# A gating layer whose three products are made of half products, with its gate mixed in place

## The chip, the cores and the metric

The kernel runs on one core of one Trainium2 chip. The metric is the device time in microseconds of one execution. Before the change the median of three runs was 1120.9 us (1119.94 to 1122.56).

## The reference

Two layers with a residual stream x of 512 tokens by 1024 features, all in float32. Layer 0 is latent attention, layer 1 a gating layer; behind each stands an MLP with a squared ReLU. The gating layer and the MLP, cut to what matters:

```python
def chunked_sgu_mixer(h, w_in, ln_g, ln_b, w_spatial, b_spatial, w_out):
    z = gelu(h @ w_in)                  # 512x1024 @ 1024x4096
    u, v = split(z, 2, axis=-1)         # 512x2048 each
    v = layer_norm(v, ln_g, ln_b)
    # per 128-token chunk and group of 256 features: lower-triangular 128x128
    mixed = einsum('gts,bcsgd->bctgd', tril(w_spatial), v in chunks) + b_spatial
    return (u * mixed) @ w_out          # 512x2048 @ 2048x1024

x = x + chunked_sgu_mixer(rms_norm(x, norm_mix[1]), ...)
x = x + square(relu(rms_norm(x, norm_ffn[i]) @ w_up)) @ w_down
```

## The kernel before

Every float32 operand of a large product is split into a high part, rounded to the matmul's float32r format, and a low part, the rest. `split` (L124) does it: the high part is a cast on ScalarE (L125), the low part a subtraction on VectorE (`low`, L122). `mm3` (L106, the matmul is L110) makes a product from three matmuls: high by high, high by low, low by high. `wtiles` hands out the tiles for the split weights, three pairs in turn (`wh`, `wl`), `raw_tile` the shared buffers in which weights land (`wr`, two of 1 MB).

**The MLPs** (`ffn`) multiply by the Winograd form of Strassen's method: a product of two matrices cut into four quarters each is made of seven half-size products instead of eight, from sums of quarters. On the left these sums are made by VectorE (`Quarters.first` and `.rest`, L313 on: turn by transposes on TensorE, L296, copies on ScalarE and VectorE, L323 and L324, sums, splits). Sums of weights are made by DMA: a block is loaded by SP's queue (`load`, L1017) and another is added into the same buffer by a DMA on POOL's queue (`add`, L1020), or by VectorE where both lie in memory (L1049, L1264). `ffn` has six weight buffers: the two `wr` and four of its own (`wb`). The up product and the down product of 1024 hidden columns are seven items each; an item is a pair `prepare` (weights and splits) and `go` (24 products of 512 columns, or 48 of 256, then what takes the banks away). The list `work` deals the items of an up product and of the down product before it alternately; the last seven down items of the first MLP stand alone. `prepare` of an item is called two items ahead of its `go`. Sums that run on in a bank (X) are added to x, or to the hidden values, while the next item already writes the other bank of the pair. During an MLP's first item the other half of its input is turned, by way of two spare banks.

**The gating layer** does not do so. For v it goes over four blocks of 512 columns (L1381 on, four banks, two weight units of 512x512 each), takes Gelu on ScalarE (L1407) and statistics on VectorE (L1408). For u there are 16 tiles of 128 features (`u_tile`), made transposed: the product, a multiplication by the norm spread over a row (`rb`, L1424), Gelu. `mixed_tile` (L1428) mixes v along the positions by four short matmuls (L1431), scales and shifts (L1436), multiplies with u and splits the result into `hid`. `gate_pieces` multiplies two such tiles with 256 rows of `w_out` in eight pieces and adds them to x (L1457). `Features` turns and splits the layer's input in two halves (`gx1`), the first at the end of the first MLP. The weights of the position mixing come by four DMAs on POOL's queue behind the norm's root (`mix_load`).

The order of instructions on each engine is made by the framework from the program's order and its dependences; an engine then takes them strictly in that order. The tile pools of the layer and of the MLPs lie in the same memory one after the other.

Of the kernel before, what the change touches and what calls it, by code (L numbers as in the profile page):

```python
# [57 lines left out]
def trunk(ctx: ExitStack, tc: tile.TileContext, a):  # L58
# [240 lines left out]
    class Features:  # L299


        def __init__(self, key, base, halves=(0, 1)):
            self.g = [gcol(key, base + k) for k in range(KD)]
            self.t = [None] * KD
            self.halves = halves
            self.left = list(halves)

        def half(self):
            h = self.left.pop(0)
            for k in range(h * 4, h * 4 + 4):  # L310
                self.t[k] = split_scaled(gpair(), turned(k), self.g[k])

    class Quarters:  # L313
# [3 lines left out]
        def __init__(self, key, base):  # L317
            self.g = [gcol(key, base + k) for k in range(KD)]

        def turn(self, e, lo, hi):  # L320
            for k in range(4):
                ps, g = turned(e * 4 + k), self.g[e * 4 + k]
# [669 lines left out]
    def ffn(layer, xq, norm, pool, after=None, last=None):  # L992
# [21 lines left out]
        spare += banks[6:8]  # L1014

        def load(t, src):
            nc.sync.dma_start(t, src)  # L1017

        def add(t, src):
            nc.gpsimd.dma_start(t, src, accum_op=ALU.add)  # L1020
# [143 lines left out]
        def down(c, sq):  # L1164
# [59 lines left out]
            def item(left, weights, sums, first, then, free=False, free_left=False, late=None):  # L1224
# [19 lines left out]
                def go():  # L1244
                    l, r = w
                    for b in range(2):
                        bs = slice(b * P, (b + 1) * P)
                        for k in range(4):
# [4 lines left out]
                            )  # L1253
                    it, u, r, done = then
# [8 lines left out]
            def t2():  # L1263
# [9 lines left out]
                item(lambda: "a22", p4, "X", False, (1, 0, r2, True), True, True),  # L1273
# [14 lines left out]
        for j, (_, go) in enumerate(work):  # L1288
            if j == 7:
# [24 lines left out]

    def after_mlp0(i, u):
        norm1.add(i, u)
        if (i, u) == (3, 0):
            gx1.half()
# [8 lines left out]
    gx = gx1.t  # L1327
    norm2 = Norm(1)
    gx2 = Quarters("norm_ffn", KD)
    with stage(7), tc.tile_pool(name="sgu", bufs=1) as sg:  # L1330
# [5 lines left out]
        v = sg.tile([P, NT, SGW], F32, name="v")  # L1336
# [3 lines left out]

        def staged(i):
            return v[:, 2 * i : 2 * i + 2, SGW - 512 :].rearrange("p a (b t) -> p a b t", t=P)
# [3 lines left out]
        bs_src = a["sgu_b_spatial"].rearrange("l g t -> (l g t)")  # L1348
        def mix_load():
            for gg in range(2):  # L1350
                nc.gpsimd.dma_start(wsp[:, gg], ws_src[:, gg * 4 : gg * 4 + 4, :])
                nc.gpsimd.dma_start(
                    v[:, 2 + gg, SGW - 512 :], bs_src[gg * 512 : (gg + 1) * 512].partition_broadcast(P)
# [27 lines left out]
        for c in range(4):  # L1381
            acc = [psum() for _ in range(NT)]
            for at, kk in enumerate(gx1.halves):
                wh, wl = unit(wview(w_in, kk * 512, 512, SGW + c * 512, 512), 4, 512)
                for i in range(NT):
                    isl = slice(i * P, (i + 1) * P)
                    for k4 in range(4):
                        k = kk * 4 + k4
                        mm3(
                            acc[i], (gx[k][0][:, isl], gx[k][1][:, isl]),  # L1390
                            (wh[:, k4, :], wl[:, k4, :]), at + k4 == 0, at * 4 + k4 == KD - 1,
                        )
                if at == 0 and c == 0:
                    gx1.half()
# [218 lines left out]
```

## Time and profile before

| | |
|---|---|
| median of 3 runs | 1120.9 us |
| profiled execution | 1121.37 us, span 1119.6 us |
| TensorE busy | 1086.3 us, 97% of the span |
| VectorE busy | 815.5 us, 73% |
| ScalarE busy | 565.9 us, 51% |
| POOL busy | 103.5 us, 9% |
| granted clock of TensorE, mean | 0.992 of 2.4 GHz |

How to read it: a matmul's listed time (390 ns for 512 columns) overlaps with the next; what one costs is the distance from start to start. The span is the first to the last instruction of the profiled execution, and its time is that span and what lies around it. The first MLP runs from about 171 to 500 us, the gating layer to about 786 us, the second MLP to the end.

### The profile page before, as it was taken

Reading aid. Unit: us, or ns where it says so; the run is one execution under the profiler, and the core shown is the slowest. Engines: PE = TensorE matmul, PEld = TensorE weight load, DVE = VectorE, ACT = ScalarE, POOL = GpSimd, SP = SyncE. Lnnn points to the kernel's source line nnn. Section 1 sums busy time; section 2 is a strip of 40 time slices with the busy share of each in tenths; the row PEclk is TensorE's granted clock in tenths of the full one; section 3 lists DMA queues with packets and bytes.
Section 4 is the critical chain, followed back from the end, with each engine's and each line's share of the span. In section 5 each row is a group of like instructions: output and inputs, shape, how many; then the busy total and the mean of one; then the engine's idle time right before and its main releaser. Section 6 shows DMA issues by size and latency. Waiting matters only on the chain.

```text
span 1119.6 us, 15248 instructions
## 1 busy us (share of the span) xinstructions
PE 1086.3 (97%) x6348; PEld 958.6 (86%) x6348; DVE 815.5 (73%) x949; ACT 565.9 (51%) x668; POOL 103.5 (9%) x137
## 2 busy tenths in 40 slices
PE   8799998999999999989999999999899999999997
PEld 6688888999999999877888888888799999998986
DVE  6988757897887888964347566568788788788753
ACT  4577636665655655554223222223675555555641
POOL 5510000001010010001000000000000001001000
PEclk9999999999999999999999999999999999999999
DMA  6121147768758768253323133223966976866431
GB/s 199 40 75 38 39 113 238 176 150 195 180 137 210 199 124 220 68 136 113 107 82 112 43 109 113 76 76 76 263 161 144 223 187 122 218 150 113 114 113 57
DMA packets 80739, 148.63 MB, mean 133 GB/s; under 512 B 4694, under 2 KB 18589, under 8 KB 80541
## 3 DMA queue, kind: packets, MB, share of 16 engines
q1 hardware_dynamic: 56588, 99.41, 26.3%
q0 software_dynamic: 24080, 48.24, 24.7%
q8 instruction: 50, 0.82, 0.3%
q14 instruction: 21, 0.16, 0.0%
HBM read 145.54 MB, written 2.10 MB: 132 GB/s over the span
## 4 chain that ended last, share of the span: by engine, by line
PE 81%; DVE 5%; DMA 5%; issue 4%; ACT 3%; POOL 0%; SPq 0%; POOLq 0%; ACTq 0%; DVEq 0%
PE ps L110 76%; DVE wl L122 2%; ACT wh L125 2%; DMA wb<-in_ffn_w_down 2%; DMA wr<-in_ffn_w_up 2%; DMA wb<-in_ffn_w_up 2%; PE ps L1431 1%; PE ps L863 1%; DVE sq L492 1%; ACT p L843 0%; PE ps L296 0%; PE ps L830 0%; PE ps L831 0%; PE ps L834 0%; PE ps L832 0%
## 5 line engine op out<-in xcount | busy, mean ns | idle before, releaser
L110 PE MATMUL ps<-g,wh 128*128 128x256 f32 (+1 forms) x2112 | 420.9, 299 | 4.4 <-DVE g L122 2.7
L110 PEld LDWEIGHTS ps<-g,wh 128*128 128x128 f32 x2112 | 339.3, 190 | 22.1 <-DVE g L122 3.6
L110 PE MATMUL ps<-g,wl 128*128 128x256 f32 (+1 forms) x1056 | 314.0, 298 | 0.6 <-DVE wl L122 0.6
L110 PE MATMUL ps<-wh,q 128*128 128x512 f32 (+1 forms) x840 | 266.2, 389 | 2.5 <-DVE x L1160 2.5
L122 DVE TENSOR_TENSOR wl<-wr,wh 128x2048 fp32r<-128x2048 f32 (+1 forms) x74 | 165.0, 2232 | 57.8 <-ACT wh L125 57.7
L110 PEld LDWEIGHTS ps<-g,wl 128*128 128x128 f32 x1056 | 199.3, 189 | 7.2 <-DVE wl L122 0.9
L122 DVE TENSOR_TENSOR wl<-wb,wh 128x2048 fp32r<-128x2048 f32 x64 | 146.6, 2290 | 65.3 <-ACT wh L125 65.2
L110 PEld LDWEIGHTS ps<-wh,q 128*128 128x128 f32 x840 | 158.0, 189 | 34.6 <-issue 2.8
L125 ACT CAST wh<-wr 128x2048 fp32r<-128x2048 f32 (+1 forms) x74 | 137.4, 1860 | 98.4 <-PE ps L110 90.2
L125 ACT CAST wh<-wb 128x2048 fp32r<-128x2048 f32 x64 | 122.0, 1906 | 102.1 <-PE ps L110 85.7
L110 PE MATMUL ps<-wl,q 128*128 128x512 f32 (+1 forms) x420 | 163.6, 390 | 0.0
L125 ACT CAST q<-sq 128x1024 fp32r<-128x1024 f32 x51 | 53.6, 1052 | 90.1 <-PE ps L110 87.5
L110 PE MATMUL ps<-wh,g 128*128 128x512 f32 x304 | 96.0, 393 | 2.0 <-ACT g L134 1.7
L110 PEld LDWEIGHTS ps<-wl,q 128*128 128x128 f32 x420 | 79.5, 189 | 14.6
L1160 DVE SCALAR_TENSOR_TENSOR x<-ps,s,x 128x512 f32<-128x512 f32 x98 | 72.6, 747 | 21.8 <-PE ps L110 21.8
L110 PE MATMUL ps<-wh,h 128*128 128x512 f32 (+1 forms) x216 | 84.7, 392 | 0.0
L110 PE MATMUL ps<-wl,h 128*128 128x512 f32 (+1 forms) x216 | 82.5, 382 | 0.0
L110 PE MATMUL ps<-wh,l 128*128 128x512 f32 (+1 forms) x216 | 82.5, 382 | 0.0
L110 PEld LDWEIGHTS ps<-wh,g 128*128 128x128 f32 x304 | 56.9, 188 | 14.9 <-ACT g L134 2.2
L122 DVE TENSOR_TENSOR q<-sq,q 128x1024 fp32r<-128x1024 f32 x51 | 62.4, 1223 | 4.9 <-ACT q L125 1.8
L110 PE MATMUL ps<-wl,g 128*128 128x512 f32 x152 | 59.2, 389 | 0.0
L1020 POOL DMA_DIRECT2D wr<-in_ffn_w_up x16 | 20.9, 1309 | 408.8 <-DVE x L1457 183.2
(229 smaller groups left out, 1229.3 us busy)
## 6 DMA issues: line engine op xcount, KB each, us to landing
wb<-in_ffn_w_up SPq DMA_DIRECT2D x18, 1024.0 KB, 6.4
wb<-in_ffn_w_down SPq DMA_DIRECT2D x17, 1024.0 KB, 5.2
wb<-in_ffn_w_down POOLq DMA_DIRECT2D x17, 1024.0 KB, 9.4
wr<-in_ffn_w_up POOLq DMA_DIRECT2D x16, 1024.0 KB, 8.4
wr<-in_sgu_w_in SPq DMA_DIRECT2D x16, 1024.0 KB, 5.6
wr<-in_ffn_w_up SPq DMA_DIRECT2D x14, 1024.0 KB, 5.5
wr<-in_ffn_w_down SPq DMA_DIRECT2D x9, 1024.0 KB, 5.1
wb<-in_ffn_w_up POOLq DMA_DIRECT2D x8, 1024.0 KB, 8.4
```

The source lines that it names most:

```text
L110: nc.tensor.matmul(out, lhsT=lhsT, rhs=rhs, start=start and t == 0, stop=stop and t == 2, **kw)
L122: return eng.tensor_sub(l, src, h.bitcast(F32))
L125: nc.scalar.copy(hl[0], src)
L492: nc.vector.tensor_tensor_reduce(out=junk, in0=x[:, i, cuts[c] * P : cuts[c + 1] * P], in1=x[:, i, cuts[c] * P : cuts[c + 1] * P], scale=1 ...
L863: nc.tensor.transpose(ps[b][:, c : c + P], pr[h, i][:, j * P : (j + 1) * P], ident)
L1020: nc.gpsimd.dma_start(t, src, accum_op=ALU.add)
L1160: nc.vector.scalar_tensor_tensor(out=xs, in0=ps, scalar=r[:, i : i + 1], in1=xs, op0=ALU.mult, op1=ALU.add)
L1431: nc.tensor.matmul(ps[:, i * P : (i + 1) * P], lhsT=v[:, i, j * P : (j + 1) * P], rhs=wt[:, j // 2, :], start=True, stop=True,)
```

## The change

All three products of the gating layer are made of seven half-size products, as in the MLPs. `Quarters` takes which half of the features comes first and gives the layer's input too (`Features` goes); its first half is turned in the middle of the first MLP's last item (`mid`). `gate(c)` makes 1024 columns of v, `other(c)` 1024 features of u, `outer` the product with `w_out`, whose seven products have two items each, one for each half of the inner dimension. That is 42 items, one list, with `prepare` two ahead, seven items of one product behind one another. The layer has three weight buffers: the two `wr` and one `wb`; two more come from v for the output. v is normalised on ScalarE (scale and bias), mixed in place, and u is multiplied by it in place (`gated`). At an MLP's beginning four banks are spare for the transposes, from its second item on two.

```diff
+        def __init__(self, key, base, first=0):
+            self.halves = (first, 1 - first)
...
-        spare += banks[6:8]
+        spare += banks[4:8]
...
-                return wview(w_up, k * 512, 512, c * 1024 + i * 512, 512)
+                return wview(w_up, xq.row(k), 512, c * 1024 + i * 512, 512)
...
+                        if b == 0 and mid is not None:
+                            mid()
...
+            if j == 1:
+                spare[:] = banks[6:8]
...
-    gx1 = Features("norm_mix", KD, (1, 0))
+    gx1 = Quarters("norm_mix", KD, 1)
...
-        ffn(0, gx0, norm, fp, after_mlp0)
+        ffn(0, gx0, norm, fp, norm1.add, None, gx1.first)
...
+        raws = Slots(
+            [raw_tile((P, 4, 512)) for _ in range(2)] + [sg.tile([P, 4, 512], F32, name=nm("wb"))]
+        )
+        banks = [psum() for _ in range(8)]
+        B, A, C, E = (banks[2 * n : 2 * n + 2] for n in range(4))
...
+        def weights(w, name, make, free, shift=0):
+
+            make()
+            w.extend(split(wtiles(4, 512, shift), s[name]))
+            if free:
+                raws.put(s.pop(name))
...
+            def p1():
+                if c:
+                    get("a", w(0, 0))
+                add(s["a"], w(0, 1))
+
+            def p2():
+                nc.vector.tensor_add(s["a"], s["a"], s["b"])
...
+            return [
+                item(X, True, "A11", "d" if c else "a",
+                     lambda: get("d" if c else "a", w(0, 0)), bool(c), end1),
+                item(Z, True, "A12", "c", lambda: get("c", w(1, 0)), True, end2),
+                item(Y, True, "N1", "a", p1, False, end5),
+                item(Y, False, "S4", "b", lambda: get("b", w(1, 1)), False, end3, p2),
+                item(X, False, "S2", "a", lambda: None, False, end6),
+                item(X, False, "S3", "b", lambda: add(s["b"], w(0, 1)), True, end7),
+                item(X, False, "A22", "a", lambda: add(s["a"], w(1, 0)), True, end4),
+            ]
...
+            def p1():
+                get("a", w(1, 0))
+                add(s["a"], w(1, 1))
...
+            return [
+                cols_item(X, True, "A11", "b", lambda: get("b", w(0, 0)), False, end1),
+                cols_item(Y, True, "S3", "a", p1, False, end5),
+                cols_item(Z, True, "A12", "c", lambda: get("c", w(0, 1)), True, end2),
+                cols_item(X, False, "S2", "a", p2, False, end6),
+                cols_item(X, False, "N1", "b", lambda: add(s["b"], w(1, 0)), True, end7),
+                cols_item(Y, False, "A22", "a", lambda: add(s["a"], w(0, 1)), True, end3),
+                cols_item(X, False, "S4", "c", lambda: get("c", w(1, 1)), True, end4),
+            ]
...
+        def gated(c, name):
+            t, m = int(name[1]) - 1, int(name[2]) - 1
+            u = uq[c][name].rearrange("p j (i t) -> p j i t", i=2)
+            nc.vector.tensor_mul(
+                u, u,
+                v[c][:, 2 * t : 2 * t + 2, m * 512 : (m + 1) * 512].rearrange(
+                    "p i (j t) -> p j i t", j=4
+                ),
+            )
...
+            product(X, True, "a11", "a", put("a", 0, 0), False, lambda: accumulate(X, 0, 0, 1))
+            product(
+                Z, True, "a12", "c", put("c", 1, 0), True, lambda: accumulate(Z, 0, 0, 1, True)
+            )
+            product(
+                Y, True, "n1", "a", sum_("a", 0, 1), False, lambda: accumulate(Y, 1, 1, -1), n1
+            )
+            product(
+                Y, False, "a12", "b", put("b", 1, 1), False, lambda: accumulate(Y, 0, 1, -1), s4, p2
+            )
+            product(
+                X, False, "a11", "a", lambda h: None, False, lambda: accumulate(X, 0, 1, -1, True)
+            )
+            product(
+                X, False, "a21", "b", sum_("b", 0, 1), True, lambda: accumulate(X, 1, 1, -1, True)
+            )
+            product(
+                X, False, "a22", "a", sum_("a", 1, 0), True, lambda: accumulate(X, 1, 0, 1, True)
+            )
...
+        work = g0[:1] + g1[:1] + g0[1:] + g1[1:] + u0 + u1 + dn
...
+        def normalised(c):
+            for i in range(NT):
+                nc.scalar.activation(
+                    v[c][:, i, :], v[c][:, i, :], AF.Identity, scale=norms["rstd"][:, i : i + 1],
+                    bias=norms["shift"][:, i : i + 1],
+                )
...
+        after(0, begin)
...
+        after(13, deviations)
...
+        after(14, lambda: normalised(0))
+        for n in range(4):
+            after(15 + n, lambda n=n: (mixed_tile(2 * n), mixed_tile(2 * n + 1)))
...
+        after(40, gx2.first)
...
+        ahead = 2
+        for prepare, _ in work[:ahead]:
+            prepare()
+        for j, (_, go) in enumerate(work):
+            go()
+            for f in then.get(j, ()):
+                f()
+            if j + ahead < len(work):
+                work[j + ahead][0]()
```

## Rows read from the trace of the kernel before

**Rows 1.** The chain that ended last, in order of time: start, us, what.

```profile
561.54 1.72 PE ps L1371 x4
...
728.32 0.89 PE ps L1431 x8
729.21 10.90 PE ps L110 x48
```

**Rows 2.** Busy time by stretch: length, PE, PEld, DVE, ACT, POOL, clock, DMA.

```profile
189.00:200.35 11.35, 9.96 (x82) 9.55 (x82) 11.35 (x12) 8.09 (x11) 1.28 (x1) 1.00 0.91 234
208.90:429.00 220.10, 220.07 (x1465) 202.83 (x1466) 177.39 (x132) 126.76 (x103) 24.50 (x19) 1.00 0.75 176
456.60:486.50 29.90, 27.45 (x122) 22.41 (x121) 24.83 (x21) 14.16 (x10) 2.58 (x2) 1.00 0.51 106
486.50:499.60 13.10, 13.10 (x52) 10.55 (x53) 10.65 (x8) 7.49 (x12) 0.00 (x0) 0.87 0.28 87
607.00:783.60 176.60, 176.60 (x852) 148.79 (x851) 117.44 (x141) 50.47 (x56) 1.41 (x2) 1.00 0.30 90
801.50:812.90 11.40, 10.14 (x76) 9.94 (x74) 10.55 (x11) 7.13 (x8) 1.29 (x1) 0.85 0.86 205
```

**Rows 3.** TensorE's waits: us in total, times, longest.

```profile
PE ps L296 <- DVE sq L324: 6.8, 2, 4.2
...
PE ps L110 <- ACT g L134: 1.7, 2, 0.9
```

**Rows 4.** Timeline of TensorE in the first MLP, first products of three items.

```profile
228.82 0.39 PE L110 MATMUL ps<-wh,q 128*128 128x512 f32 x1
...
234.29 0.40 PE L110 MATMUL ps<-g,wh 128*128 128x256 f32 x2
...
239.94 0.40 PE L110 MATMUL ps<-wh,q 128*128 128x512 f32 x1
```

**Rows 5.** Groups of instructions by line and shape: busy us, mean ns, idle before.

```profile
L122 DVE TENSOR_TENSOR wl<-wr,wh 128x2048 fp32r<-128x2048 f32 x70 | 160.2, 2289 | 57.8 <-ACT wh L125 57.7
...
L125 ACT CAST wh<-wr 128x2048 fp32r<-128x2048 f32 x70 | 133.3, 1906 | 98.4 <-PE ps L110 90.2 <-DMA wr<-in_ffn_w_up 6.9 <-issue 1.3
...
L122 DVE TENSOR_TENSOR q<-sq,q 128x1024 fp32r<-128x1024 f32 x51 | 62.4, 1223 | 4.9 <-ACT q L125 1.8
...
L1077 DVE TENSOR_TENSOR sq<-sq,ps 128x512 f32<-128x512 f32 x48 | 32.6, 682 | 4.4 <-PE ps L110 3.2
...
L1408 DVE BATCH_NORM_STATS2 stats<-v 128x6 f32<-128x512 f32 x16 | 11.1, 694 | 20.9 <-ACT v L1407 20.7
```

**Rows 6.** Timeline of the first MLP's last items: an add and what follows.

```profile
471.12 1.28 POOL L1020 DMA_DIRECT2D wb<-in_ffn_w_down  x1 [43.21 <-DVE wl L122]
...
479.67 1.91 ACT L125 CAST wh<-wb 128x2048 fp32r<-128x2048 f32 x1 [5.58 <-DMA wb<-in_ffn_w_down]
...
481.61 2.29 DVE L122 TENSOR_TENSOR wl<-wb,wh 128x2048 fp32r<-128x2048 f32 x1 [4.44 <-ACT wh L125]
...
486.50 0.47 PE L110 MATMUL ps<-wh,q 128*128 128x512 f32 x1 [2.45 <-DVE x L1160]
```

**Rows 7.** DMA issues: how many, KB each, median us to landing.

```profile
wb<-in_ffn_w_down POOLq DMA_DIRECT2D x17, 1024.0 KB, 9.4
wr<-in_ffn_w_up POOLq DMA_DIRECT2D x16, 1024.0 KB, 8.4
wr<-in_sgu_w_in SPq DMA_DIRECT2D x16, 1024.0 KB, 5.6
```

**Rows 8.** Timeline of the second MLP's beginning.

```profile
795.97 1.90 ACT L125 CAST wh<-wb 128x2048 fp32r<-128x2048 f32 x1 [4.54 <-DMA wb<-in_ffn_w_up]
...
797.90 2.29 DVE L122 TENSOR_TENSOR wl<-wb,wh 128x2048 fp32r<-128x2048 f32 x1 [5.86 <-ACT wh L125]
...
800.65 1.10 PE L296 MATMUL ps<-ident,x 128*128 128x128 f32 x8 [4.15 <-DVE sq L324]
```

**Rows 9.** Line L1020, the adds into a shared buffer: duration ns min/median/max.

```profile
L1020 POOL DMA_DIRECT2D wr<-in_ffn_w_up x16: 1277/1293/1521, 152.7 to 1019.1; - x16
```

More of the change, by code (lines that the diff above doesn't have):

```diff
@@ L990, in put, with load, add, ffn @@
             self.free.append(t)
-    def ffn(layer, xq, norm, pool, after=None, last=None):
+    def load(t, src):
+        nc.sync.dma_start(t, src)
+    def add(t, src):
+        nc.gpsimd.dma_start(t, src, accum_op=ALU.add)
+    def ffn(layer, xq, norm, pool, after=None, last=None, mid=None):
         w_up, w_dn = a["ffn_w_up"][layer], a["ffn_w_down"][layer]
@@ L1222, in s4, with item @@
                 return "a12"
-            def item(left, weights, sums, first, then, free=False, free_left=False, late=None):
+            def item(
+                left, weights, sums, first, then, free=False, free_left=False, late=None, mid=None,
+            ):
                 w = []
@@ new lines, in get, with rows_item, prepare, go @@
+        def get(name, src):
+            s[name] = raws.get()
+            load(s[name], src)
+        def weights(w, name, make, free, shift=0):
[3 more added lines that the diff above has]
+                raws.put(s.pop(name))
+        def rows_item(acc, first, left, name, make, free, end, late=None):
+            w, l = [], []
+            def prepare():
+                l.extend(left())
+                weights(w, name, make, free)
+                if late is not None:
+                    late()
+            def go():
+                for b in range(2):
+                    bs = slice(b * P, (b + 1) * P)
+                    for k in range(4):
+                        mm3(
+                            acc[b], (l[0][:, k, bs], l[1][:, k, bs]), (w[0][:, k, :], w[1][:, k, :]),
+                            first and k == 0, k == 3, skip_group_check=True,
+                        )
+                end()
+            return prepare, go
@@ new lines, in cols_item, with go @@
+        def cols_item(acc, first, right, name, make, free, end):
+            w = []
+            def go():
+                r = getattr(gx1, right)
+                for m in range(4):
+                    ms = slice(m * P, (m + 1) * P)
+                    out = acc[m // 2][:, (m % 2) * H : (m % 2 + 1) * H]
+                    for k in range(4):
+                        mm3(
+                            out, (w[0][:, k, ms], w[1][:, k, ms]), (r[0][:, k, :], r[1][:, k, :]),
+                            first and k == 0 and m % 2 == 0, k == 3, skip_group_check=True,
+                        )
+                end()
+            return lambda: weights(w, name, make, free, 16), go
@@ L1466, in trunk @@
[L1466 to L1472 removed]
+        def gated(c, name):
[5 more added lines that the diff above has]
+                    "p i (j t) -> p j i t", j=4
+                ),
+            )
@@ new lines, in trunk, with after, begin @@
+        g0, g1 = gate(0, A, E, C), gate(1, B, E, C)
+        u0, u1 = other(0, A, E, C), other(1, C, E, A)
+        dn = outer(A, C, E)
+        work = g0[:1] + g1[:1] + g0[1:] + g1[1:] + u0 + u1 + dn
+        then = {}
+        def after(n, f):
+            then.setdefault(n, []).append(f)
+        def begin():
+            gx1.rest(*(uq[0][t] for t in ("a11", "a12", "a21")))
+            r = inv_sqrt(norm1.mean())
+            with tc.issue_after(root[0].ins):
+                mix_load()
+            norms["r"], norms["nr"] = r, small()
```

322 lines of the change are left out of this document (202 added, 120 removed).

## The prediction

> **What bounds the kernel now.** I read the chain of waits first, then busy time by stretch, then TensorE's waits. In the gating layer TensorE never stops: 48 products of 512 columns take 10.90 us again and again [rows 1], and in the stretch 607 to 783.6 us it is busy for all 176.60 us, VectorE for 117.44, ScalarE for 50.47 [rows 2]. So in this stage fewer products are less time, as long as nothing else ends last. The stretch of the first MLP, already made of half products, is just as full (220.07 of 220.10 us) with VectorE at 177.39 [rows 2]: half products can keep TensorE fed, but there the lists of two products are dealt alternately, so what one item leaves to the next of its own list has twice the time. The new layer runs its seven items straight after one another. TensorE's waits over the kernel are few [rows 3].
>
> **The products.** Before: 4 column blocks x 4 row tiles x 8 slices x 3 terms = 384 products for v, 16 x 8 x 3 = 384 for u, 8 x 8 x 2 x 3 = 384 for the output: 1152, or 24 groups of 48 at 10.90 us [rows 1]: 261.6 us. After: 42 items. The 28 with rows on the output (gate and output) have 24 products of 512 columns; in the MLP such an item runs from 228.82 to 234.29, 5.47 us. The 14 for u have 48 of 256 columns, as from 234.29 to 239.94, 5.65 us [rows 4]. 28 x 5.47 + 14 x 5.65 = 232.3 us. **Minus 29.3 us**, all on the path. The spread-out norm becomes one full-precision product instead of two short ones: two products with the same ones, again 512 columns, took 1.72 us [rows 1], so 0.86 against 2 x 0.23: plus 0.4. Transposes and position mixing keep their number.
>
> **VectorE and ScalarE.** Weight splits go from 24 to 42, each 1.91 us of ScalarE and 2.29 of VectorE; half-size operations on VectorE take 1.22, those on one bank 0.68 [rows 5]. Gate: 14 x 2.29, 2 weight sums x 2.29, 12 bank adds, 16 statistics of 0.69, some 15 of the rest for splitting the second half of the input and for the shifts: 32 + 5 + 8 + 11 + 15 = 71 of about 80 us of TensorE. u: 32 + 5 + 8 (adds) + 9 (norm rows) + 12 (mixed tiles) + 10 (gating in place) = 76 of 93 (14 x 5.65 and 16 mixed tiles of 0.89 [rows 1]), comfortable. Output: 14 x (2.29 + 1.22) + 2 x 2.29 + 8 x 1.22 + 14 x 0.68 + 5 for the next MLP's first half = 78 of 78. Normalising v moves to ScalarE, which has room. The nearest row for so full a VectorE is the end of the first MLP, seven output items alone: it lost one wait of 2.45 us [rows 6]. For the output I take **plus 3** (0 to 6).
>
> **Waits for weights.** This is the disputed term. A buffer is loaded, split, then another block is added into it by a DMA on POOL's queue, and split again. Add and second split are seen once without a second list between: add issued 471.12, cast 479.67, low part 481.61 + 2.29 = 483.90, so 12.8 us from issue to use [rows 6]; the medians of these adds are 8.4 and 9.4, that of a plain load 5.6 [rows 7]. With only three weight buffers in the layer instead of six the chains are short:
> - S4 to S3 of a gate share b: two items, 10.9 us. Besides, the sum of a and b (2.29) reads b before the add. A split can be at most 10.9 - 4.2 = 6.7 us early (three pairs of split tiles), so the cycle is between 0 and 4.2 us late. In the first gate half the backlog of splitting the input leaves it near the late end: 3.5. In the second: 0.6.
> - N1 of the second gate half loads into the buffer that S3 of the first frees, then adds: 5.6 + 8.4 + 4.2 = 18.2 us, in three items (16.4): 2.2 with the usual lead gone. The S3 item of u's first half has the same chain: 2.0.
> - At the layer's start the two A11 items cover 10.9 us; VectorE has some 10 us of input splits, three weight splits and evacuations to do by the fourth item: 3.3 late.
>
> The first gate's N1 add is costed at nothing: its buffer is free before the layer begins, so it can be issued ahead of the norm's root on POOL. Queued behind the root, the mixing's four loads and their two masks it would come too late, which the upper end of 24 covers. Queued behind a late cast on ScalarE are the evacuations of the banks; behind the low part on VectorE, the bank adds that release X. In [rows 6] that is how a late add became TensorE's wait for x. Sum 11.6, taken as **plus 11.6** (3 if the leads hold, 24 if none does). In u the mixed tiles stretch the later items and give the chains room: nothing there.
>
> **The clock.** After the wait of 2.45 us, the stretch 486.5 to 499.6 was granted 0.87: a quarter of it, 3.4 us, at 1.2 GHz, which costs 1.7 us; after 4.15 us [rows 8], 801.5 to 812.9 had 0.85, as much; after the other long wait, 2.65 us, 189 to 200.35 stayed at 1.00 [rows 2]. So two of three. With three such waits new, **plus 3.4** (0 to 6).
>
> **What goes.** At the layer's start the waits for scaled input (1.7 [rows 3]) go, **minus 1.7**, and at the two MLP beginnings transposes waited 6.8 us in all for banks [rows 3]: four banks remove these, but the next item's weights are not earlier: cast begun 795.97, low part over at about 800.2, when the transposes ran at 800.65 [rows 8]. VectorE's queue gets shorter by the turned copies only. I take **minus 3** in the first MLP (0 to 5). In the second the gain (0 to 5) meets a new lateness: the layer holds both shared weight buffers to its last items, and the MLP's S3 weights need 5.6 + 8.4 + 4.2 = 18.2 us from the release, with some 13 to 18 there. Zero, from minus 5 to plus 5.
>
> **The sum:** -29.3 + 0.4 + 3 + 11.6 + 3.4 - 1.7 - 3 = -15.6 against the profiled execution's 1121.37 us (span 1119.6 and 1.8 around it): 1105.8. It stands 0.5 above the median of the runs, 1120.9, so 1105.3, rounded to **1105.0 us**.
>
> **A rule against it.** The 16 adds of one row took 1.28 to 1.52 us to issue on POOL, median 1.29 [rows 9], beside a VectorE that is 80% busy in the MLP's stretch [rows 2]. The Trainium skill, SBUF — State Buffer, section "SBUF: two separate sides", warns that transfers issued from GpSimd can starve for descriptors while VectorE holds their shared port. By it the sum would be rival 4's; the trace, with its narrow spread of issue times, does not show such a hold.
>
> **Rivals.**
> 1. The leads hold (no wait for weights, no new fall of the clock): -29.3 + 0.4 + 3 - 1.7 - 3 = -30.6, 1090 us. For it: the MLP stretch without a gap. Against: its alternating lists. 0.17.
> 2. VectorE becomes the bound. In the stretch of the output items alone it did not pass 83% (24.83 of 29.90 us [rows 2]). At that share gate and output take 71/0.83 = 86 and 78/0.83 = 94 us instead of 80 and 78: 22 in place of 11.6 + 3: -8.2, 1112.7 us. 0.11.
> 3. Slower: every item whose weights come by an added DMA (six in the gate halves, six in u's) is late by 2.5 us and followed by the half clock, 1.7: 12 x 4.2 = 50 in place of 15.0: 1140 us. It decides from 2.6 us per item: 12 x 2.6 is what the other terms without 15.0 leave as gain. The clock's two falls speak for it, the leads and the mixed tiles against. 0.06. The Trainium skill, TensorE: Matmul & The Clock Gate, "HAM oscillation", has this very pattern: a wait for a transfer before each block drops the clock each time. Here two of three long waits did so.
> 4. POOL's issues are held for the length of a VectorE operation, 2.29 us, at each of those twelve adds: 27 us more, 1132 us. 0.03, since none of the present issues shows it. This is what the rule of the SBUF page would give.
> 5. The change does not bring what it says at the MLPs: the copies stay queued behind the late weight split and four banks gain nothing: 1108 us, inside my range.
>
> **How the numbers follow.** My forecast, rival 5 with it, gets 0.63, rivals 1 to 4 0.17, 0.11, 0.06 and 0.03. Its own bounds, taken half way (the terms are unlikely to fall on one side together), give 1094 to 1116; to hold 8 in 10 the range goes down past rival 1 and takes in rival 2: 1088 to 1117. About 0.2%, 2.2 us, is what can be told from no change. Faster: the forecast, 1 and nearly all of 2: 0.87; same: 0.04; slower: 0.09.
>
> **What would show it.** Right: about 42 items at 5.47 or 5.65 us, TensorE's waits for low parts and banks of 10 to 15 us between the first gate item and the first u items, one or two stretches at a clock below 1.00, the layer some 13 us shorter. Wrong: no waits there (rival 1), waits spread over all of gate and output on VectorE (2), or waits on late casts with the clock falling in each item (3); POOL issues of over 2 us (4); a wait of over 5 us at the second MLP's third item.

## The result and the profile after

The changed kernel takes 1136.15 us (median of four, 1133.39 to 1138.21) beside 1121.73 us before on the same chip: 1.0127 times, interval 1.0097 to 1.0158. That is 31 us over the predicted 1105.0, above the range, and on the other side of no change. The profiled execution took 1138.21 us, its span 1136.5; the mean granted clock of TensorE was 0.973, where it was 0.992 before.

The page of the changed kernel, busy time over the span (PE is TensorE, PEld its weight loads, DVE VectorE, ACT ScalarE; SPq below is the queue of the plain loads):

```profile
PE 1074.1 (95%) x6540; PEld 957.3 (84%) x6540; DVE 866.0 (76%) x947; ACT 628.8 (55%) x714; POOL 129.0 (11%) x155
```

TensorE's busy time fell by 12 us only, from 1086.3, and the span grew by 17. Where, is read from the starts of the stages in both traces. The layer begins with its first product (`wh,g`), the second MLP with the first `g,wh` of 256 columns; the last column is the prediction's sum, cut at the same places (layer: -29.3 + 0.4 + 3 + 11.6 + 3.4 - 1.7):

| us | before | after | difference | predicted |
|---|---|---|---|---|
| to the layer's first product | 501.11 | 502.95 | +1.84 | -3 |
| the layer | 285.56 | 290.41 | +4.85 | -12.6 |
| second MLP to the end | 332.91 | 343.15 | +10.23 | 0 |
| span | 1119.6 | 1136.5 | +16.9 | -15.6 |

So all three stages missed, the layer by 17.5 us, the second MLP by 10.2, the first by 4.8. These are single executions: 1.1 us of the first row's +1.84 stand ahead of the first MLP already (its first `g,wh` starts at 176.71 and 177.77), in work that the change does not touch. TensorE's waits over the whole kernel (us in total, times, longest), to be held against [rows 3]:

```profile
PE ps L110 <- ACT wh L125: 9.7, 3, 4.9
PE ps L296 <- DVE x L1640: 7.1, 1, 7.1
PE ps L110 <- DVE g L122: 6.4, 3, 3.2
PE ps L110 <- DVE wl L122: 6.1, 5, 1.6
PE ps L110 <- ACT g L125: 4.4, 3, 2.9
PE ps L1605 <- ACT v L1740: 3.5, 1, 3.5
```

The wait for banks (`sq` L324, 6.8 us) is gone as the change means it to. In its place stand waits for high and low parts of weights, and for what is queued behind these. Busy time of the changed kernel in stretches of 10 us, columns as in [rows 2] and behind the clock the busy share of the 16 DMA engines and GB/s:

```profile
520.00:530.00 10.00, 9.49 (x30) 7.65 (x31) 9.90 (x10) 3.52 (x4) 0.00 (x0) 0.70 0.01 2
...
550.00:560.00 10.00, 9.64 (x34) 7.51 (x35) 8.31 (x14) 6.98 (x7) 1.28 (x1) 0.83 0.74 213
560.00:570.00 10.00, 5.06 (x21) 3.88 (x20) 4.87 (x10) 3.60 (x4) 0.00 (x0) 0.85 0.90 215
570.00:580.00 10.00, 10.00 (x37) 8.04 (x36) 7.93 (x7) 3.26 (x4) 0.00 (x0) 0.81 0.01 2
...
800.00:810.00 10.00, 3.40 (x18) 3.40 (x19) 7.48 (x6) 8.52 (x13) 0.00 (x0) 0.66 0.24 85
```

Seven of the 17 stretches from 510 to 680 stand below 1.00, and the second MLP's beginning at 0.66; before, all of the layer's stood at 1.00. TensorE does not stop where VectorE is full: in 560 to 570 both have some 5 us and ScalarE less. What they wait for is a DMA, as the timeline of all engines shows at three places (start, duration, what, idle time before and its releaser):

```profile
550.34 5.47 SPq L986 DMA_DIRECT2D wr<-in_sgu_w_in  x2
556.19 1.28 POOL L989 DMA_DIRECT2D wr<-in_sgu_w_in  x1 [13.41 <-DMA wr<-in_sgu_w_in]
567.09 1.90 ACT L125 CAST wh<-wr 128x2048 fp32r<-128x2048 f32 x1 [5.43 <-DMA wr<-in_sgu_w_in]
569.04 1.22 PE L110 MATMUL ps<-wh,g 128*128 128x512 f32 x2 [4.94 <-ACT wh L125]
...
713.86 0.37 SPq L986 DMA_DIRECT2D v<-in_sgu_w_out  x1
725.14 1.90 ACT L125 CAST wh<-v 128x2048 fp32r<-128x2048 f32 x1 [6.45 <-DMA v<-in_sgu_w_out]
727.09 0.92 PE L110 MATMUL ps<-wh,g 128*128 128x512 f32 x2 [3.83 <-ACT wh L125]
...
783.92 2.29 SPq L986 DMA_DIRECT2D wb<-in_ffn_w_up  x3
786.23 1.30 POOL L989 DMA_DIRECT2D wr<-in_ffn_w_up  x1 [22.35 <-DMA wr<-in_ffn_w_up]
786.25 0.59 SPq L986 DMA_DIRECT2D wb<-in_ffn_w_down  x1
800.59 1.90 ACT L125 CAST wh<-wr 128x2048 fp32r<-128x2048 f32 x1 [10.04 <-DMA wr<-in_ffn_w_up]
802.52 2.29 DVE L122 TENSOR_TENSOR wl<-wr,wh 128x2048 fp32r<-128x2048 f32 x1 [8.98 <-ACT wh L125]
805.86 0.68 DVE L1640 TENSOR_TENSOR x<-x,ps 128x512 f32<-128x512 f32 x1
806.60 2.98 PE L296 MATMUL ps<-ident,x 128*128 128x128 f32 x13 [7.09 <-DVE x L1640]
```

Items go by the names of the diff; in the gate they run A11, A12, N1, S4, S2, S3, A22. At 550 us the buffer that S3 of the first gate half frees is loaded; the add into it is issued when that has landed, the cast follows 10.9 us after the add, and TensorE stands for it 4.94 us: N1's first product, which the framework put two products into A12. At 714 a block of the output's weights is loaded into a buffer that v gives up only after gating (L1617, over at 713.80); two other loads and an add are under way beside it, and the cast follows 11.3 us after the issue. At 780 a shared buffer comes free so late that the second MLP's add runs beside four loads, 14.4 us from issue to cast; the low part waits for that cast, an add to x waits in VectorE's queue behind the low part, and the transposes for the banks that this add empties.

A bound that the prediction does not name is the DMA engines themselves. Their share in the changed kernel while the second MLP's add ran, and over gate and u:

```profile
786.00:801.00 15.00, 13.51 (x91) 11.99 (x89) 4.75 (x7) 3.21 (x6) 1.30 (x1) 1.00 1.06 312
...
502.95:706.75 203.80, 185.06 (x1166) 164.57 (x1167) 145.23 (x146) 106.61 (x107) 23.93 (x21) 0.94 0.60 146
```

And over gate and u in run 3 below, with a fourth buffer:

```profile
504.99:697.40 192.41, 180.62 (x1166) 160.64 (x1167) 146.03 (x147) 107.04 (x108) 23.30 (x21) 0.99 0.66 162
```

Where transfers come together the DMA engines are full (1.06; the view counts a packet where it starts). Over the stage they are not: 0.60 in the changed kernel, 0.66 in the faster run 3, and 0.75 in the first MLP, where TensorE never stops [rows 2]. So their rate alone does not set the time.

### The profile page after: what moved, and what is told of

Its sections match the earlier page's. It is cut to its first block, busy times and chain, and to the rows that moved or that the text cites. A ratio compares the mean times of both kernels' runs of the same rounds, so it can differ in the third digit from the quotient of the medians.

```text
span 1136.5 us, 15747 instructions
## 1 busy us (share of the span) xinstructions
PE 1074.1 (95%) x6540; PEld 957.3 (84%) x6540; DVE 866.0 (76%) x947; ACT 628.8 (55%) x714; POOL 129.0 (11%) x155
## 5 line engine op out<-in xcount | busy, mean ns | idle before, releaser
L110 PEld LDWEIGHTS ps<-g,wh 128*128 128x128 f32 x2304 | 362.3, 191 | 17.8 <-DVE g L122 4.4
L110 PEld LDWEIGHTS ps<-g,wl 128*128 128x128 f32 x1152 | 218.8, 190 | 5.5 <-DVE wl L122 4.3
L122 DVE TENSOR_TENSOR wl<-wb,wh 128x2048 fp32r<-128x2048 f32 x74 | 169.5, 2290 | 62.8 <-ACT wh L125 62.7
L125 ACT CAST wh<-wb 128x2048 fp32r<-128x2048 f32 x74 | 141.1, 1907 | 109.6 <-PE ps L110 82.5
L110 PE MATMUL ps<-wh,g 128*128 128x512 f32 x496 | 164.5, 408 | 15.6 <-ACT wh L125 9.7
L110 PEld LDWEIGHTS ps<-wh,g 128*128 128x128 f32 x496 | 97.0, 197 | 41.6 <-ACT wh L125 11.6
L110 PE MATMUL ps<-wl,g 128*128 128x512 f32 x248 | 101.0, 407 | 2.6 <-DVE wl L122 2.6
L1154 DVE SCALAR_TENSOR_TENSOR x<-ps,s,x 128x512 f32<-128x512 f32 x98 | 72.7, 747 | 20.9 <-PE ps L110 20.9
L110 PEld LDWEIGHTS ps<-wl,g 128*128 128x128 f32 x248 | 48.7, 197 | 14.1 <-DVE wl L122 3.3
L989 POOL DMA_DIRECT2D wr<-in_ffn_w_up x16 | 20.9, 1308 | 265.8 <-DMA wr<-in_ffn_w_up 103.9
L989 POOL DMA_DIRECT2D wb<-in_ffn_w_down x17 | 21.9, 1291 | 131.3 <-DVE wl L122 129.5
L1071 DVE TENSOR_TENSOR sq<-sq,ps 128x512 f32<-128x512 f32 x48 | 32.6, 683 | 2.5 <-PE ps L110 1.3
```

The source lines that it names most:

```text
L110: nc.tensor.matmul(out, lhsT=lhsT, rhs=rhs, start=start and t == 0, stop=stop and t == 2, **kw)
L122: return eng.tensor_sub(l, src, h.bitcast(F32))
L125: nc.scalar.copy(hl[0], src)
L1071: both(name, lambda t, j: nc.vector.tensor_add(t, t, pv(acc[sums][j])))
L1154: nc.vector.scalar_tensor_tensor(out=xs, in0=ps, scalar=r[:, i : i + 1], in1=xs, op0=ALU.mult, op1=ALU.add)
```

## The experiments

The theory from here on: the weights' chains through too few buffers (load, add, cast, low part) set the pace. Its rivals: VectorE is the bound; the half clock is the loss by itself; the queues' order is (a late cast or product ahead of work that is ready). The table gives all runs; gate + u, output and second MLP are stage lengths, read as above (the output begins with the first `wh,g` behind u). Each is from one profiled execution; run 2's was the longest of its twelve, run 4's the second shortest of its ten, run 12's the shortest of its seven.

| kernel | median us | ratio to before | gate + u | output | 2nd MLP |
|---|---|---|---|---|---|
| changed | 1136.15 | 1.0127 [1.0097, 1.0158] | 203.8 | 86.6 | 343.1 |
| 1 no adds | 1108.52 | 0.9877 [0.9863, 0.9892] | 180.5 | 80.6 | 343.2 |
| 2 four banks alone | 1121.84 | 1.0001 [0.9989, 1.0014] | 285.6 with the output | | 334.4 |
| 3 fourth buffer | 1108.71 | 0.9883 [0.9860, 0.9906] | 192.4 | 80.4 | 329.6 |
| 4 fourth buffer from the output on | 1122.86 | 1.0003 [0.9988, 1.0019] | 204.6 | 80.4 | 329.6 |
| 5 filler | 1139.47 | 1.0148 [1.0126, 1.0169] | 205.2 | 85.9 | 342.8 |
| 6 own buffer for S3 | 1112.25 | 0.9903 [0.9884, 0.9923] | 193.3 | 80.4 | 329.6 |
| 7 copies first, from 6 | 1111.28 | 0.9911 [0.9895, 0.9927] | 193.5 | 80.4 | 329.5 |
| 8 copies first, from 3 | 1109.66 | 0.9888 [0.9857, 0.9919] | 192.1 | 80.4 | 329.9 |
| 9 own buffer for A22, from 6 | 1118.28 | 0.9963 [0.9947, 0.9979] | 198.1 | 82.4 | 329.5 |
| 10 items in order, from changed | 1136.38 | 1.0125 [1.0105, 1.0146] | 200.8 | 87.2 | 344.3 |
| 11 ends first, from 6 | 1108.32 | 0.9875 [0.9854, 0.9897] | 188.8 | 80.4 | 329.4 |
| 12 ends first, from 9 | 1116.86 | 0.9953 [0.9937, 0.9970] | 193.5 | 83.2 | 329.4 |

**1. The layer without its adds.** All 18 adds into weight buffers of the layer are left out (its weight sums lack those blocks); loads, splits, products and VectorE's work stay.

```diff
-                add(s["a"], w(0, 1))
+                no_add(s["a"], w(0, 1))
```

> The changed kernel with the adding DMAs of the gating layer left out (all 18 of them: N1, S3, A22 of the gate halves, S3, N1, A22 of u's, six of the output), so its weight sums are not the reference's. VectorE, ScalarE and TensorE do the same work. Theory A (waits for added weights, each followed by the half clock, cost the layer its gain): the waits before S3 and N1 of the gate and S3 of u, some 11 us, go, and most of the 12 us of half clock in the layer: 1116 us (1110 to 1121), the wait of 7 us and what follows at the second MLP's beginning stays. Rival B (VectorE is so full that it is the bound): 1136 us, within 4. Rival C (the loads, not the adds, are late): half of A, about 1127 us.

Measured 1108.52 us, below theory A's range: more came back than it asked for. TensorE's waits from 500 to 765 us, and the sum of the stretches 500 to 780 (columns PE, PEld, DVE, ACT, POOL):

```profile
PE ps L110 <- DVE g L122: 2.4, 1, 2.4
PE ps L110 <- ACT wh L125: 1.3, 2, 1.1
```

```profile
sum 280.00, PE 268.93 PEld 236.69 DVE 227.00 ACT 161.75 POOL 9.22; mean PE 9.60 PEld 8.45 DVE 8.11 ACT 5.78 POOL 0.33
```

The layer takes 261.1 us, 29.3 less than in the changed kernel. With VectorE at 81% (227.00 of 280) TensorE waits 3.9 us: VectorE is not the bound. Rival C is out as well, though leaving out the adds also takes 18 transfers from beside the loads: the waits for added data and the crowding of the transfers go together here. The second MLP's wait stays (343.2): the layer's adds are not its cause.

**2. Four banks alone**, in the kernel before.

```diff
-        spare += banks[6:8]
+        spare += banks[4:8]
...
+            if j == 1:
+                spare[:] = banks[6:8]
```

> The kernel before with the four spare banks at the MLPs' beginnings alone. Theory A, from the first MLP of the changed kernel, where the wait for a bank gave way to one of 3.2 us for a split on VectorE and 3 us of half clock: no gain, 1121 to 1123 us. Rival (my prediction's term): 3 to 5 us less, 1117 us.

1121.84 us, no difference, as theory A had it. Its timeline at the two MLP beginnings:

```profile
196.60 0.39 PE L110 MATMUL ps<-g,wh 128*128 128x256 f32 x1 [3.17 <-DVE g L122]
...
806.08 0.79 PE L110 MATMUL ps<-g,wh 128*128 128x256 f32 x2 [2.70 <-ACT g L125]
809.76 0.58 PE L110 MATMUL ps<-g,wh 128*128 128x256 f32 x1 [2.89 <-DVE g L122]
```

The waits for banks (2.65 and 4.15 before) are gone, and the next wait takes their place: the input's sums and splits.

**3. A fourth weight buffer**, from room that narrower split tiles give (2064 columns for 2112; the norm row uses the full-precision ones, so one constant goes), and at the output the buffers are handed out so that the shared ones come free first.

```diff
-            [raw_tile((P, 4, 512)) for _ in range(2)] + [sg.tile([P, 4, 512], F32, name=nm("wb"))]
+            [raw_tile((P, 4, 512)) for _ in range(2)] + [sg.tile([P, 4, 512], F32, name=nm("wb")) for _ in range(2)]
...
+        after(26, output_buffers)
```

> The changed kernel with a fourth weight buffer in the layer (the room comes from shorter split tiles, 2064 for 2112 columns, and from the rounded ones), in the output handed out so that the two shared buffers carry only the c blocks and are free ten items before the layer's end. Theory A2 (the second MLP begins late because a shared buffer is released late, and the chains load then add need a buffer earlier): the wait of 4.9 us before N1, the 1.6 before u's S3, the 3.8 in the output and the 7.1 and what follows at the second MLP go, with their half clock: 1114 us (1108 to 1120). Rival B (VectorE is the bound): no more than 4 us less, 1132 us.

1108.71 us: 1.2% faster than before, at the lower end of theory A2's range. Its waits in the layer, from 504 to 778 us:

```profile
PE ps L110 <- ACT v L1463: 5.6, 4, 2.4
PE ps L110 <- DVE g L122: 2.9, 1, 2.9
PE ps L110 <- DVE wl L122: 2.7, 2, 1.3
```

The layer takes 272.8 us, 12.7 less than before, where 12.6 was predicted; the second MLP 3.3 less. That the layer's totals meet is in part luck: its waits (12.8 us, 11.3 more than before, 12.9 forecast) and its half clock (one fall, some 1.6 us, 3.4 forecast) are 3 us smaller, and the products' gain is smaller by as much. The fourth buffer and the order in which the output hands its buffers out were not tried apart.

**4. The fourth buffer only from the output on.** Gate and u have three, as in the changed kernel.

> The changed kernel with a fourth weight buffer that is used only from the layer's output product on; gate and u have three buffers as in the changed kernel. Two losses are to be told apart: the waits in gate and u with the half clock behind them, and the late weights of the output and of the second MLP's beginning. Theory A (both cost, each in its own place): the wait before N1 of the second gate half (4.94 us) and the ones of u (1.61 and 3.46) stay, the output's 3.83 + 0.89 and the second MLP's 7.09 go, and the time lies between the changed kernel and the one with four buffers throughout: 1119 us, 1113 to 1125. Theory B (the gate's chains alone made the loss, the late weights behind them are their echo): 1130 us or more, the wait of 7 us before the second MLP's third item stays. Theory C (the second MLP's late weights alone): 1110 us or less, as with four buffers throughout, though the gate's waits stay.

1122.86 us, between the two, as theory A of this run had it, some 4 us above its figure. In the timeline the gate's wait stays (4.94 before), and at the second MLP nothing over 1.03 us is left:

```profile
570.75 1.07 PE L110 MATMUL ps<-wh,g 128*128 128x512 f32 x2 [4.24 <-ACT wh L125]
...
789.21 0.50 PE L110 MATMUL ps<-g,wh 128*128 128x256 f32 x2 [1.03 <-ACT g L125]
```

By the stage lengths the fourth buffer is worth 12.2 us in gate and u (204.6 to 192.4), 6.2 in the output (86.6 to 80.4) and 13.5 in the second MLP (343.1 to 329.6); the last two are its worth together with the order of handing out. These are single executions: by the medians it is 14.2 us from run 4 to run 3 and 13.3 from the changed kernel to run 4, 27.4 in all and not 31.9.

**5. Filler.** In the changed kernel 30 products that nothing reads are put where TensorE waits before S3 and N1.

```diff
+        after(5, lambda: filler(10))
+        after(8, lambda: filler(20))
```

> The changed kernel with 10 products of 512 columns that nothing reads after the gate's item S2 of the first half and 20 after its item A12 and S4 (0.227 us each at full clock: 2.3 and 4.5 us), placed where TensorE waits 1.10 + 1.35 us and 4.94 us. No weight comes earlier by it. Theory A (the half clock follows TensorE's idle time): the two waits shrink by the filler's time, the granted clock of 545 to 580 us stays above 0.95 where the changed kernel has 0.81 to 0.85, and the time is 2 to 5 us less, about 1132.5 us. Theory B (the clock falls for some other reason, such as what the other engines do): the clock falls as before and the time is the same or up to 3 us longer.

1139.47 us. Stretches, and the filler and the next long wait in the timeline:

```profile
550.00:560.00 10.00, 7.84 (x25) 5.72 (x25) 6.11 (x7) 6.24 (x6) 1.28 (x1) 0.83 0.58 156
560.00:570.00 10.00, 10.00 (x44) 7.89 (x43) 7.03 (x20) 2.00 (x2) 0.00 (x0) 1.00 1.02 268
570.00:580.00 10.00, 10.00 (x46) 8.29 (x45) 8.75 (x8) 5.04 (x6) 0.00 (x0) 1.00 0.00 0
```

```profile
571.81 4.70 PE L1773 MATMUL ps<-g 128*128 128x512 f32 x20
...
598.51 0.50 PE L110 MATMUL ps<-wh,g 128*128 128x512 f32 x1 [3.83 <-ACT v L1464]
```

The half of theory A that speaks of the clock holds behind the second filler: 0.85 and 0.81 became 1.00 where TensorE had work. The first filler did not do it: waits of 1.35 and 2.16 us stand around S3 instead of 1.10 and 1.35, and 550 to 560 stays at 0.83. The half on the time falls: gate and u take 205.2 us after 203.8. In the second half TensorE waits 1.52 and 3.83 us at S4 and S3, where the changed kernel had none and 1.28 + 0.99. This does not show that the half clock is free. Over the layer the waits fell from 23.4 to 20.9 us and the time at 1.2 GHz from 30.7 to 20.5 us, worth some 4 us by the reckoning of the clock's term further down, and the 30 products of filler take 6.8 us themselves: what they save they cost. Whether the half clock runs in time that the weights' chains take anyway stays open.

**6. S3's weights in a buffer of their own**, on top of run 3, whose waits stand around S3.

```diff
+                get("t", w(1, 1))
+                add(s["t"], w(0, 1))
...
-                item(X, False, "S3", "b", lambda: add(s["b"], w(0, 1)), True, end7),
+                item(X, False, "S3", "t", lambda: None, True, end7),
```

> Four weight buffers as in the run before it, and the weights of the gate's item S3 are loaded and added in a buffer of their own instead of by an add into the block that S4 and the weight sum have to have read first. Theory A (that add's chain holds S3): TensorE's waits before S3, 1.15 + 1.34 us in the first half and 2.37 + 0.57 + 1.34 + 1.51 around the second, go, with the stretch of lower clock at 550 to 560 us; 1101 us, 1097 to 1105. Theory B (VectorE's and ScalarE's backlog at the layer's start holds the splits, whichever buffer they read): the waits of the first half stay within 1 us, those of the second may go, 1106 to 1110 us.

1112.25 us, nothing gained, and above the times of both theories. The timeline at S3:

```profile
553.71 1.90 ACT L125 CAST wh<-wr 128x2048 fp32r<-128x2048 f32 x1 [4.38 <-DMA wr<-in_sgu_w_in]
555.51 0.58 ACT L1463 COPY v<-ps 128x512 f32<-128x512 f32 x1
556.15 0.80 PE L110 MATMUL ps<-wh,g 128*128 128x512 f32 x1 [3.60 <-ACT v L1463]
```

S3's weights are early now. But ScalarE stands at the cast for A22, an item further on, whose add has not landed, and the copy that empties S3's second bank is queued behind it. Neither theory had named this.

**7 and 8. The copies first:** the cast of A22's weights behind the two copies that empty S2's banks, in the kernels of 6 and 3.

```diff
-                item(X, False, "A22", "a", lambda: add(s["a"], w(1, 0)), True, end4),
+                behind(item(X, False, "A22", "a", lambda: add(s["a"], w(1, 0)), True, end4)),
```

> The run before it (four weight buffers, S3's weights in a buffer of their own), and in both gate halves the cast of A22's weights is issued on ScalarE behind the two copies that empty S2's banks, where it stood between them. Theory A (the second copy, queued behind a cast that waits for its DMA, holds TensorE before S3): the waits of 3.60 and 3.18 us before S3 go with the half clock behind them; 6.8 us of waits and up to 3.4 of clock, 1103 us, 1099 to 1106. Theory B (the weights' DMA chain sets the pace and the copy only shows it): the waits come back one item later, before A22, as waits for its low part, and the time stays within 3 us of the run before it, 1109 to 1114.

> The same order of ScalarE's queue in the kernel with four weight buffers in which S3's weights are still added into the buffer of S4. Theory A: the waits on the copies (1.15 + 2.37 us in the first half, 1.51 in the second) go, the ones on S3's low part (1.34 twice) stay; 1104 us, 1101 to 1107. Theory B (the chain of the add into S4's buffer comes next): they turn into longer waits on S3's or A22's low part; 1106 to 1111.

1111.28 and 1109.66 us, within 1 us of the kernels they are made from: theory B's times. In 7 the wait is an item later, before A22 itself, and now VectorE's queue stands, a bank add behind a low part:

```profile
554.24 1.90 ACT L125 CAST wh<-wr 128x2048 fp32r<-128x2048 f32 x1 [3.44 <-DMA wr<-in_sgu_w_in]
...
556.17 2.29 DVE L122 TENSOR_TENSOR wl<-wr,wh 128x2048 fp32r<-128x2048 f32 x1 [4.65 <-ACT wh L125]
...
558.99 1.26 DVE L1479 TENSOR_TENSOR v<-v,ps 128x512 f32<-128x512 f32 x2
...
559.80 0.77 PE L110 MATMUL ps<-wh,g 128*128 128x512 f32 x1 [3.17 <-DVE v L1479]
```

**9. A22 without its add:** the block is loaded plainly and VectorE adds it.

```diff
+                get("e", w(1, 0))
...
+                nc.vector.tensor_add(s["a"], s["a"], s["e"])
...
-                item(X, False, "A22", "a", lambda: add(s["a"], w(1, 0)), True, end4),
+                item(X, False, "A22", "a", p4, True, end4),
```

> Four weight buffers and a buffer of its own for S3, as two runs before; A22's block of the gate halves is now loaded plainly into a third buffer of its own and added to the sum by VectorE (2.29 us) instead of by an added DMA, which can only be issued when the sum has been split. Theory A (A22's added DMA, issued late by the chain on its buffer, is what the casts on ScalarE and the sums on VectorE stand behind): the waits of 3.60 and 3.18 us at S3, and their like one item later, go with the half clock behind them; 1104 us, 1100 to 1107. Theory B (the loads themselves are late, since two more plain loads per half share the DMA engines): new waits on a cast that waits for a load, 1109 us or more.

1118.28 us, a time of theory B. Theory A's waits at S3 and A22 of the first half are gone. But the next add, for N1 of the second half, is now the late one (an add, not a plain load as theory B had it), and more stands behind its cast: A22's Gelu on ScalarE, behind that the statistics and shifts on VectorE, which hold A12's bank.

```profile
556.03 1.28 POOL L987 DMA_DIRECT2D wb<-in_sgu_w_in  x1 [2.88 <-DMA wb<-in_sgu_w_in]
565.43 1.90 ACT L125 CAST wh<-wb 128x2048 fp32r<-128x2048 f32 x1 [10.26 <-DMA wb<-in_sgu_w_in]
569.85 2.05 PE L110 MATMUL ps<-wh,g 128*128 128x512 f32 x4 [7.48 <-DVE Bt L1389]
```

**10 to 12. The order of the queues by itself.** In 10, the changed kernel, and in 11 and 12 an item's products are issued behind those of the item before; in 11 and 12 (from 6 and 9) the gate's next casts and low parts also wait in the queues behind all that the last item leaves to ScalarE and VectorE.

```diff
+                with behind_products():
...
+                    for last in tail.values():
+                        order.enter_context(tc.issue_after(last.ins))
                     work[j + ahead][0]()
```

> The changed kernel, in which each item's products in the layer are issued on TensorE behind the last product of the item before. In the changed kernel the framework puts the first product of the second gate half's N1 two products into A12, and TensorE stands there 4.94 us for a weight that is due 5 us later; in the output an item has its first product ahead of the item before it in the same way (3.83 + 0.89 us). Theory A (this order costs the time by which the weight's lateness passes what is due): the wait before N1 falls to about 2 to 3 us (its low part is behind the late cast as well), the output's to under 2; 1130 us, 1126 to 1133. Theory B (the weights' chains set the pace, the order only shows it): the waits stand elsewhere with the same sum, 1134 us or more.

> The kernel with four buffers and one of its own for S3, with two rules for the order of the queues: each item's products behind the last one of the item before (TensorE), and in the gate halves the casts and low parts of later items' weights behind the bank copies, bank adds, Gelus and statistics of the item just done (ScalarE, VectorE). Theory A (late casts and low parts cost only through what is queued behind them): the waits of 3.60 and 3.18 us before S3 go, and none of over 1.5 us comes in the gate halves behind the layer's start; 1104 us, 1100 to 1107. Theory B (the add's DMA chain sets the pace): the waits come back before A22 as waits for its own high or low part, 1109 us or more.

> The same two rules in the kernel in which A22's block is loaded into a buffer of its own as well and added by VectorE. Theory A: the wait of 7.48 us behind a Gelu that stood behind the next N1's late cast goes with the half clock behind it (two stretches of 10 us at 0.81 and 0.68); 1107 us, 1102 to 1111. Theory B: the late cast of that N1 is then waited for by its own item, 3 us or more, 1112 to 1118.

Run 10: 1136.38 us, no gain, as theory B had it. A12 runs through now, but N1 then waits 3.01 us for its low part, and the mixed tiles wait longer for v (4.73 after 3.46); the layer's waits sum to 23.4 us in both kernels. Run 11: 1108.32 us, between the two theories. The two waits of over 3 us are gone and what is left is small, gate and u 4.5 us shorter than in 6; the time gained 4 us of the 8 that theory A asked for, at the edge of what the two intervals tell apart. It is level with run 3, by another way. Run 12: 1116.86 us, in theory B's range, though the wait of 7.48 us is gone and none of 3 us or more, which theory B names, has come (the layer's longest is 1.97); why these two kernels with one more load per half stay above run 6 is open. The longest wait of the gate halves behind the layer's start, in the timeline of 10 and of 11:

```profile
570.17 0.50 PE L110 MATMUL ps<-wl,g 128*128 128x512 f32 x1 [3.01 <-DVE wl L123]
```

```profile
596.25 0.50 PE L110 MATMUL ps<-wl,g 128*128 128x512 f32 x1 [1.82 <-DVE wl L123]
```

## Why the prediction was wrong

Of the layer's 17.5 us some 9 are waits (23.4 us, less 1.5 before, for 11.6 + 3 - 1.7) and some 9 the clock; 10.2 more came at the second MLP's beginning. Term by term:

- **Products, -29.3 us:** held. In run 1 the layer is 24.4 us shorter than before. The sum for it is -29.3 + 0.4, plus 3.9 of waits, less 1.5 of waits before (0.83 + 0.30 + 0.33; the other 0.89 us of the 1.7 for scaled input stand ahead of the layer's first product): -26.5; one stretch at 0.84 (520 to 530) adds up to 1.6. It is right within some 2 us.
- **Waits for weights, +11.6:** 18.7 in gate and u, over it but inside the bounds of 3 to 24. The layer's start was right (3.3; 0.88 + 2.50), so were S3 of the first half (3.5; 2.45) and of u (2.0; 1.61). Mis-sized were N1 of the second half (2.2, by its own sum 18.2 - 16.4 = 1.8; 4.94), because the add took 10.9 us to the cast and not 8.4, S3 of the second half (0.6; 2.27), and the mixed tiles, where "nothing there" was 3.5 us of waiting for v, normalised late.
- **The clock, +3.4 (0 to 6):** the term of the layer that was most mis-sized. What the layer's other terms leave is 4.85 + 29.3 - 0.4 - 23.4 + 1.5 = 11.8 us (23.4 are all waits of its stretch). By the granted clock TensorE had 30.7 us at 1.2 GHz in five falls, 5.4 of them waits: (30.7 - 5.4) / 2 = 12.7. The step that failed: "three such waits new", of which "two of three" fall. There were five falls, one of them at two short waits in a row (1.10 + 1.35 us, 550 to 560 at 0.83). What the falls cost by themselves is not shown: in run 10 the layer has the same 23.4 us of waits and 13.7 us at 1.2 GHz instead of 30.7, and is 2.5 us shorter in one execution, with the median the same.
- **The output's VectorE, +3:** the size was near (4.7 us of waits), by luck, for the cause was wrong: run 3 has the same work on VectorE, and its output takes 80.4 us without a long wait. It was a load into v's buffer, 11.3 us from issue to cast, which I had not costed.
- **Second MLP's beginning, 0 (-5 to +5):** +10.2, the step with the largest miss for its bounds and the one that failed most plainly. "5.6 + 8.4 + 4.2 = 18.2 us from the release, with some 13 to 18 there": from the release (low part over, 777.83 + 2.29) to the end of the next low part (804.81) it took 24.7, since the add ran beside four loads, 14.4 us. And I costed the wait, not what queues behind it, though I had named that very queue ("behind the low part on VectorE, the bank adds that release X"). Its sign of being wrong, "a wait of over 5 us at the second MLP's third item", came (7.09). That the lateness is the whole of it is shown by run 3: with the buffers early this stage is 3.3 us shorter than before.
- **First MLP's four banks, -3:** nothing, as rival 5 had it (run 2). The step that failed took the wait that ended last for the only one; the input's splits were 3 us behind it.
- **Rivals.** Rival 3 came nearest in time (1140), with the right links (added weights, then half clock) and the wrong count: not twelve late items at 4.2 us but five falls in the layer, and a third of the miss behind it. By the Trainium skill, TensorE: Matmul & The Clock Gate, "HAM oscillation", a wait for a transfer before each block of products brings the slow clock each time; this trace agrees in the layer (five falls, each at 2.4 us or more of waits), while run 5 had a wait of 2.71 us without a fall. Rival 1, leads that hold, is what the layer shows in run 1 only, without the adds. Rival 2 fell with run 1. Rival 4 fell with the issues themselves, which answer to [rows 9]; the duration in ns is least, median, most:

```profile
L989 POOL DMA_DIRECT2D wr<-in_sgu_w_in x10: 1274/1292/1335, 495.0 to 671.9; - x10
```

- **The range:** half of the sum of the upper bounds is 13 us and makes 1118 where 1116 is written; 1136 lies above either.

In one sentence: the sum came near a kernel with a fourth buffer (layer 12.7 us shorter, 1108.7 us in all), while with three a buffer came late in each of gate and u, output and second MLP; 12.2, 6.2 and 13.5 us by the stage lengths of single executions, 27.4 in all by the medians.

## What to carry to other kernels

Where half products take sums of weights, follow each buffer from its release over load, add, cast and low part to its use, with the add's time under load (here 8 to 14 us, not its median), and go on past the stage's end into the next stage's first items. A cast that waits for its DMA holds everything behind it on a strict queue, also the evacuations of items that have their weights (run 6); here moving it on ScalarE alone brought nothing (runs 7 and 8), moving it on ScalarE, VectorE and TensorE together some 4 us with four buffers (run 11), and the order of the products alone nothing with three (run 10). A wait that is filled, hidden or reordered (runs 2, 5, 6, 7, 10) often only names the next one.

## What the runs showed of the hardware

An added DMA of 1 MB is not one number: 8.4 to 9.4 us in the median before [rows 7], 9.6 in the layer of the changed kernel, from issue to cast 10.9 with two loads beside it, one after the other, and 14.4 beside four, where plain loads took 5.5:

```profile
wr<-in_sgu_w_in SPq DMA_DIRECT2D x11, 1024.0 KB, 5.5
wr<-in_sgu_w_in POOLq DMA_DIRECT2D x10, 1024.0 KB, 9.6
```

Plain loads stretch in the same way: two of the four beside the second MLP's add took 15.4 and 16.8 us to land, with the DMA engines full. That the transfers beside one another are what slowed them was not tried by itself.

The length of a wait did not tell whether the clock falls. An early item of the layer waits 2.0 to 3.2 us in the changed kernel and in runs 1 and 3 to 12. The clock fell at that wait or within 1.6 us of its end in nine of these twelve executions, and stayed at 1.00 after 2.94 us in run 3, 2.71 in run 5 and 2.48 in run 10. Waits of 1.10 and 1.35 us with 0.5 us of work between them brought a fall in the changed kernel; the like of them brought none in runs 3, 8 and 10.
